# Reordering in three places of a two-layer sparse-attention block: x tiles turned earlier, one softmax moved, casts held

## The chip, the cores and the metric

The kernel runs on one core of a Trainium2 chip. The metric is the device time of one execution in microseconds (us); the time before is the median of three runs, 749.46 us (749.03 to 749.6). The core has a matrix engine (TensorE; PE in the profile, PEld for its weight loads), VectorE (DVE), ScalarE (ACT), GpSimd (POOL) and a queue that issues most DMAs (SP). GpSimd issues DMAs too, among them the accumulating ones. Each engine takes its instructions in the order of its own queue.

## The reference

Two layers are applied to 528 tokens (16 meta tokens and 512 of x) of width 1024. Each projects the normalised tokens to several parts, lets an indexer choose 128 keys for each query, attends to these, adds a pooled branch, gates both and adds an output product to its input:

```
def hybrid_layer(x, ...):
    h = rms_norm(x, norm_g)
    proj = h @ w_in           # q, k, v, gate_a, u_b, gate_b, q_idx, k_idx, w_idx, merge
    q = rope(rms_norm(q)); k = rope(rms_norm(k)); q_idx = rope(q_idx); k_idx = rope(k_idx)
    score = sum_heads(relu(q_idx . k_idx) * w_idx)        # keys after the query's chunk left out
    sel   = the 128 best keys of each query
    attn  = softmax(q . k[sel] / 8) @ v[sel]              # 8 heads, one k and v
    y_a = (attn * silu(gate_a)) @ w_a
    y_b = (pool(u_b) * silu(gate_b)) @ w_b
    g_a, g_b = sigmoid(merge)
    return x + (g_a * y_a + g_b * y_b) @ w_out
```

Only the 512 tokens of x are returned.

## The kernel before, in words

**Precision.** Matrix products run in a fast format that rounds its inputs. To keep the precision, an operand is split into a high part (a cast, on ScalarE) and a low part (the difference, on VectorE or GpSimd), and each product is three: high by high, high by low, low by high. So each chunk of weights needs casts (`w<-raw`) and subtractions (`w<-raw,w`) before its product; raw weights lie in four buffers, split ones in eight. The state of the tokens is kept transposed: `RES` (channels by tokens), its normalised form `NF`, and the split form `hhi`, `hlo`.

**Order of the work.** TensorE's and VectorE's instructions stand in the order in which the program issues them. ScalarE's, GpSimd's and SP's order is chosen by a planner, which estimates when each could run; `tc.issue_after(x)` makes it put an instruction behind `x`. The program issues its groups of matmuls one after the other, and after each group `group_done()` (from line 357) issues what is due: items put off with `later(fn, n)` until n groups are over, one item of weight preparation (`prep_q`), and steps of `fill`, a queue of Python generators that holds the index scores and the attention. A generator's `yield` ends a step. So where a `yield` stands in the attention decides between which matmul groups an instruction comes.

**The start.** x arrives in four tiles of 128 tokens (`xt`), the first two at once, the last two (t = 3, 4) issued behind the first weights. `x_half` takes their sums of squares (ScalarE), and GpSimd makes `rstd`, the reciprocal root. `x_turned` (16 transposes for the last two tiles, into banks `a`) fills `RES`. `norm_half` turns `rstd` along the tokens with two more transposes and multiplies, which gives eight blocks `nf` on VectorE, then `hhi` (ScalarE) and `hlo`. In layer 0 the first three tiles (meta, 1, 2) go ahead: keys and values of these (`plain_trio`), index queries of tile 1 (`tok_group`, 24 matmuls), *then* the transposes of tiles 3 and 4, a fold of the meta keys, index queries of tile 2, with the second `norm_half` in the middle of its matmuls (`hooks[1]`), and then keys of tile 3 and 4 (`plain_group`), which read `nf` straight.

**Attention.** `attention` (from line 746) works on 16 units u = 4i + j: query tile i (0 to 3), two heads each. `logits(u)` makes scores on TensorE into the four banks `a`; `soft(u)` adds the mask on VectorE, which reads the scores out of the banks (`lt<-a,sc`), takes the running minimum `mn`, and then takes the exponential on ScalarE (L780); `scale(u)` normalises; `turn(u)` transposes, into banks `a` again; `values(u)` multiplies by v. The steps run between the matmul groups of the gates' products (`mix_gates`). For u of 13 and above, `soft(u)` is issued in the same step as `logits(u)`, below that one step later. Unit 12 is the first of the last query tile, whose scores take two banks for each head, so all four.

**Products of seven.** The gates and part of the last output product run as `group_of_products` (from line 979): a 2 x 2 block product in seven products instead of eight, with sums of the inputs (`sums_of_h`, `sums_of_merged`) and of the weights (`mixed_prep`, nine items i0 to i8: casts, low parts, sums on VectorE, and an accumulating DMA `raw<-s` from GpSimd). The seven products are a11, a12, s2, s1, s3, s4, a22 in turn, over three banks `d`. After the first, ScalarE copies the bank out (`p`) before the third may add to it.

**The end.** In layer 1, the products with `w_a` give `ta`; its sum with `zb` is cast to `hhi` (L1405). `rows(c, t, w)` computes one tile of 128 tokens by 256 output channels: two transposes of `RES`, a copy `rt` of these (L1479), 24 matmuls, and on VectorE the sum `ot`, which a DMA writes out. Column block 0 and three tiles of block 1 are done so; the sums for the last two blocks are made meanwhile: `first`, `sums` and `lows` for each of four k, and `fourth`, `last_high` and `last_low`, whose result is wanted only by the seventh product (a22). Then `mix_out` runs two groups of seven products, with the last `rows` between.

Of the kernel before, what the change touches and what calls it, by code (L numbers as in the profile page):

```python
# [36 lines left out]
LAG1 = 2  # L37
# [53 lines left out]
def tile_block(ctx: ExitStack, tc: tile.TileContext, x, meta, w_in, pool_w, w_a, w_b, w_out, rows, hgain, c_tab, out):  # L91
    nc = tc.nc
    act, gp = nc.scalar, nc.gpsimd
# [149 lines left out]
        else:  # L243
            prep_q.extend((lambda: high(0), second, lambda: low(1)))

    added = [None]

    def first_sum(c):
        if c in mixed:
# [2 lines left out]
    def mixed_prep(c):  # L252

        r0, r1 = raws[c]
        blk = {"a11": r0[:, 0], "a21": r0[:, 1], "a12": r1[:, 0], "a22": r1[:, 1]}
        src = {"a11": "a11", "a12": "a12", "a22": "a22", "s3": "a21", "s2": "s2", "s1": "a11", "s4": "a12"}
        ops = ready[c]

        def hi(n):
            t = w_tile().rearrange("p (s k e) -> p s k e", s=2, k=4)  # L260
            ops[n] = t
            act.copy(t[:, 0], blk[src[n]])  # L262

        def lo(n):
            dve.tensor_sub(ops[n][:, 1], blk[src[n]], f(ops[n][:, 0]))

        def i0():
            hi("a12")

        def i1():  # L270
            lo("a12")
            blk["s2"] = tmp.tile([128, 544], F32, tag="L", name="s2", bufs=LB)[:, :512].rearrange(
                "p (k e) -> p k e", k=4)
            dve.tensor_add(blk["s2"], blk["a21"], blk["a22"])
            gp.dma_start(blk["a12"], blk["s2"], accum_op=OP.add)  # L275
            hi("a11")

        def i2():
            lo("a11")
            dve.tensor_sub(blk["a11"], blk["s2"], blk["a11"])  # L280

        def i3():
            hi("s2")

        def i4():
            lo("s2")
            hi("s1")

        def i5():
            lo("s1")  # L290
            hi("s3")

        def i6():
            lo("s3")
            hi("s4")
            first_sum(c + 1)

        def i7():
            lo("s4")
            hi("a22")  # L300

        def i8():
            lo("a22")
            del raws[c]
            w_load()

        def counted(fn):
            def item():
                fn()
                progress[c] += 1  # L310
            return item

        progress[c] = 0
        return [counted(fn) for fn in (i0, i1, i2, i3, i4, i5, i6, i7, i8)]
# [19 lines left out]
    def later(fn, n=2):  # L334
        pend.append((count[0] + n, fn))
# [410 lines left out]
    def attention(ensure, later_rate):  # L746
# [95 lines left out]
        for u in range(-1, 17):  # L842
            while u == 4 and not SIL["ready"]:
                yield
            if u == 7:
                rate[0] = later_rate
            if u + 1 < 16:
                logits(u + 1)
            if 0 <= u < 16:
                scale(u)  # L850
            if 13 <= u + 1 < 16:
                soft(u + 1)
            yield
            if u + 1 < 13:
                soft(u + 1)
            if u >= 1:
                turned.append(u - 1)
                if u % 4 == 0 or (u > 8 and u % 2 == 0):
                    while turned:
                        values(turned.pop(0))  # L860
                if u % 4 == 0:
                    meta_values(u // 4 - 1)
            yield
            if u >= 1 and u % 4 == 0:
                gated(u // 4 - 1)
            if 0 <= u < 16:
                turn(u)
                if u % 4 == 3:
                    meta_turn(u // 4)
            yield  # L870
# [280 lines left out]
    rstd = one.tile([128, 5], F32, name="rstd0")  # L1151
# [39 lines left out]
    tp = bank("d")  # L1191
# [7 lines left out]
    dve.tensor_scalar(psc, parT[:, 24:32], 0.5, None, op0=OP.mult)  # L1199
    dve.tensor_reduce(fold, ident.rearrange("p (j c) -> p c j", j=4), axis=AX.X, op=OP.add)  # L1200
    tables(0, True)
    hooks = {0: lambda: None, 1: lambda: ends.append(norm_half(0, 1, rstd, LAG1))}
    ends = []

    for l in range(2):
# [16 lines left out]
        w = chunk()  # L1222
        W["use"] += 1
        if l == 0:
            squared = x_half(1, halved)
        for t in (1, 2):
            later(lambda t=t, ps=pss[t]: kv_post(l, t, ps), 1)
        later(lambda ps=pss[0]: meta_sum(ps, KV, lambda total: kv_post(l, 0, total)), 1)
# [1 line left out]
        for what, t in (("q", 1), ("q", 2), ("k", 3), ("k", 4), ("q", 3), ("q", 4)):  # L1230
            if what == "k":
                ps = plain_group(t, raws[kv])
                later(lambda t=t, ps=ps: kv_post(l, t, ps), 1)
            else:
                index_queries(t, 0, w, hooks[1] if (l, t) in ((0, 2), (1, 1)) else None)
                if (l, t) == (0, 1):
                    x_turned(1, squared)
            group_done()
            if (what, t) == ("k", 3):
                w_prep_enqueue(True, None if l else ends[0])  # L1240
            if (what, t) == ("k", 4):
                del raws[kv]
                w_load()
# [228 lines left out]
        else:  # L1472
            def rows(c, t, w, half=lambda: None):
# [2 lines left out]
                for b in range(2):  # L1476
                    pe.transpose(tp[:, b * 128:(b + 1) * 128], RES[0][:, 2 * c + b, s:s + 128], ident)
                rt = tmp.tile([128, HB], F32, tag="tt", name="rt", bufs=6)
                act.copy(rt[:, :256], tp[:, :256])  # L1479
                ps = bank("d")  # L1480
                steps = [(jj, k) for k in range(KT) for jj in range(3)]
                if c == 0 and t == 1:
# [17 lines left out]
            w = chunk()  # L1500
            for t in range(1, 4):
                rows(1, t, w)
            for k in range(4):
                fourth(k)
                last_high(k)
            later(lambda: [last_low(k) for k in (0, 1)], 2)
            later(lambda: [last_low(k) for k in (2, 3)], 3)
            mix_out(operands)
            rows(1, 4, w, flush)

# [51 lines left out]
```

## Time and profile before

| | |
|---|---|
| median of three runs | 749.46 us |
| profiled execution | 749.96 us, of which the span (first to last instruction) 748.1 |
| busy: TensorE, its weight loads | 735.4 us (98%), 705.9 (94%) |
| busy: VectorE, ScalarE, GpSimd | 589.5 (79%), 482.3 (64%), 243.9 (33%) |
| DMA | 106.41 MB, 142 GB/s on average |
| granted TensorE clock | 0.999 of full speed |

A row of the timeline gives the start (us), the duration, engine, line, operation, `out<-in` by the program's names, the shape, a count where neighbours are merged, and in brackets how long the engine was idle before and what ended that. Line 62 is a helper through which all instructions of TensorE and VectorE go, so these are told apart by their tiles. A row of the list of waits gives who waited for whom: us in total, times, the longest.

### The profile page before, as it was taken

What the parts mean: (1) busy time and instruction counts of PE and PEld (TensorE: products, weight loads), DVE (VectorE), ACT (ScalarE), POOL (GpSimd) and SP (SyncE); (2) the same over time, 40 slices, a digit from 0 to 9 for tenths busy, and PEclk for the clock granted to TensorE, in tenths of its full rate; (3) what the DMA queues carried; (4) which work ended last, traced back from release to release, by engine and by line L of the source; (5) the groups of instructions that cost most, each with busy time, mean ns of one, the idle gap of its engine ahead of it and who ended that gap; (6) DMA issues with size and microseconds to landing.
All of it is one profiled execution on the core that took longest, in us unless ns stands there. A gap on an engine that the chain in (4) does not pass through costs nothing.

```text
span 748.1 us, 16060 instructions
## 1 busy us (share of the span) xinstructions
PE 735.4 (98%) x5949; PEld 705.9 (94%) x5949; DVE 589.5 (79%) x1500; ACT 482.3 (64%) x1099; POOL 243.9 (33%) x320
## 2 busy tenths in 40 slices
PE   9999999999999999999999999999999999999998
PEld 8899998999999999999999989998899999999997
DVE  6876998998898785794358669999989977678674
ACT  6669745657688786543245796557577877865543
POOL 3642074721222211063346411755031231106200
PEclk9999999999999999999999999999999999999999
DMA  8766764964654523643422687669364644548732
GB/s 264 229 169 159 167 143 113 229 147 93 146 110 116 124 59 99 179 149 115 142 87 85 173 179 195 154 153 220 84 141 108 140 93 91 128 122 241 182 88 71
DMA packets 103566, 106.41 MB, mean 142 GB/s; under 512 B 5008, under 2 KB 83632, under 8 KB 103488
## 3 DMA queue, kind: packets, MB, share of 16 engines
q1 hardware_dynamic: 91888, 74.89, 33.1%
q0 software_dynamic: 11520, 30.41, 22.8%
q8 instruction: 46, 0.75, 0.4%
q14 instruction: 32, 0.26, 0.1%
q10 hardware_dynamic: 80, 0.08, 0.0%
HBM read 66.41 MB, written 8.55 MB: 100 GB/s over the span
## 4 chain that ended last, share of the span: by engine, by line
PE 71%; DVE 14%; ACT 5%; DMA 5%; issue 2%; POOL 1%; SPq 1%; DVEq 0%; POOLq 0%; ACTq 0%
PE d L62 57%; PE a L62 10%; PE v L62 4%; DVE sc L62 3%; DVE w L62 2%; DVE m L62 2%; DMA xt<-in_x_dram 2%; DMA raw<-in_w_out_dram 1%; ACT lt L780 1%; ACT w L262 1%; DMA raw<-s 1%; DVE t L62 1%; DMA w<-raw 1%; DVE s L62 1%; POOL hlo L1407 1%
## 5 line engine op out<-in xcount | busy, mean ns | idle before, releaser
L62 PE MATMUL d<-hhi,w 128*128 128x256 f32 (+3 forms) x1392 | 279.3, 292 | 1.3 <-DVE w L62 0.7
L62 PEld LDWEIGHTS d<-hhi,w 128*128 128x128 f32 x1392 | 222.3, 188 | 5.6 <-DVE w L62 1.6
L62 PE MATMUL d<-hlo,w 128*128 128x256 f32 (+3 forms) x696 | 189.8, 289 | 0.0
L62 PEld LDWEIGHTS d<-hlo,w 128*128 128x128 f32 x696 | 131.2, 189 | 1.4 <-issue 0.2
L62 DVE TENSOR_TENSOR w<-raw,w 128x512 fp32r<-128x512 f32 (+1 forms) x156 | 120.7, 784 | 3.9 <-ACT w L262 3.9
L62 PE MATMUL d<-hsum,w 128*128 128x264 f32 (+1 forms) x720 | 95.4, 285 | 0.5 <-ACT p L1006 0.4
L62 PEld LDWEIGHTS d<-hsum,w 128*128 128x128 f32 x720 | 89.4, 188 | 1.5 <-ACT p L1006 0.8
L262 ACT CAST w<-raw 128x512 fp32r<-128x512 f32 x132 | 76.5, 622 | 18.0 <-DVE raw L62 9.5
L62 PE MATMUL d<-w,hhi 128*128 128x256 f32 x576 | 86.1, 287 | 1.4 <-ACT hhi L1405 1.1
L62 PEld LDWEIGHTS d<-w,hhi 128*128 128x128 f32 x576 | 74.7, 188 | 6.3 <-ACT hhi L1405 1.3
L250 POOL DMA_DIRECT2D raw<-raw x22 | 19.9, 903 | 117.8 <-DMA raw<-in_w_in_dram 66.6
L62 DVE MATCH_REPLACE8 sc<-m,sc 128x400 f32<-128x400 f32 (+2 forms) x100 | 54.3, 548 | 0.0
L220 POOL DMA_DIRECT2D w<-raw x34 | 31.6, 945 | 68.6 <-ACT w L219 46.2
L62 DVE MAX8 m<-sc 128x8 f32<-128x400 f32 (+2 forms) x100 | 52.6, 556 | 0.8
L275 POOL DMA_DIRECT2D raw<-s x22 | 19.3, 875 | 84.9 <-issue 23.4
L780 ACT ACTIVATE lt<-lt,mn,NR 128x144 f32<-128x144 f32 (+3 forms) x64 | 42.3, 664 | 6.3 <-DVE mn L62 6.0
L62 DVE SCALAR_TENSOR_TENSOR sc<-r,wsg,sc 128x144 f32<-128x144 f32 (+3 forms) x56 | 32.4, 582 | 17.3 <-ACT r L704 15.0
L62 PE MATMUL d<-w,hlo 128*128 128x256 f32 x288 | 45.7, 281 | 0.0
L62 PE MATMUL d<-mhi,w 128*128 128x272 f32 (+2 forms) x192 | 45.3, 324 | 0.0
L1407 POOL TENSOR_TENSOR hlo<-ta,hhi 128x256 fp32r<-128x256 f32 (+1 forms) x28 | 26.8, 966 | 46.6 <-PE d L62 34.4
L795 POOL TENSOR_SCALAR pm<-lt,rs 128x16 f32<-128x16 f32 x48 | 24.5, 549 | 52.5 <-DVE rs L62 47.9
L667 POOL TENSOR_TENSOR t<-t,t 128x256 f32<-128x256 f32 (+1 forms) x34 | 32.1, 944 | 28.5 <-DVE t L62 28.2
(245 smaller groups left out, 1560.6 us busy)
## 6 DMA issues: line engine op xcount, KB each, us to landing
raw<-in_w_in_dram SPq DMA_DIRECT2D x88, 256.0 KB, 3.5
w<-raw POOLq DMA_DIRECT2D x34, 512.0 KB, 5.9
raw<-in_w_in_dram SPq DMA_DIRECT2D x32, 512.0 KB, 4.5
raw<-in_w_out_dram SPq DMA_DIRECT2D x12, 512.0 KB, 3.7
raw<-raw POOLq DMA_DIRECT2D x22, 256.0 KB, 4.0
raw<-s POOLq DMA_DIRECT2D x22, 256.0 KB, 3.3
kept<-res SPq DMA_DIRECT2D x16, 264.0 KB, 2.5
res<-kept SPq DMA_DIRECT2D x16, 264.0 KB, 6.1
```

What stands on the lines that cost most here:

```text
L62: return fn(*a, **k)
L220: gp.dma_start(t, raws[c][s], accum_op=OP.add)
L250: gp.dma_start(raws[c][0][:, 1], raws[c][0][:, 0], accum_op=OP.add)
L262: act.copy(t[:, 0], blk[src[n]])
L275: gp.dma_start(blk["a12"], blk["s2"], accum_op=OP.add)
L667: added[0] = gp.tensor_tensor(t1[:m, :256], t1[:m, :256], t2[:m, :256], op=OP.add).ins
L780: act.activation(L[hh][:, :n], L[hh][:, :n], AF.Exp, scale=NR[:, i, h:h + 1], bias=mn[:, hh:hh + 1], accum_out=sm[:, hh:hh + 1])
L795: (gp if j < 3 else dve).tensor_scalar(pms[i][:, 2 * j + hh, :], L[hh][:, 0:16], rs[:, hh:hh + 1], None, op0=OP.mult)
L1407: pool_end = gp.tensor_sub(hlo[:, j, a:a + n], d, f(hhi[:, j, a:a + n]))
```

## The change

1. **x tiles.** In layer 0 `x_turned(1, ...)` (the 16 transposes) is issued directly after `x_half`, ahead of the first index queries. `norm_half(0, 1, ...)` is issued right after these queries and no longer inside the second ones.
2. **Softmax.** The bound in `attention` goes from 13 to 12: `soft(12)` is issued in the step of `logits(12)`, in both layers. On VectorE its four passes and the product on `mn` come ahead of a sum `c`, a low part `w` and a subtraction of the weight preparation.
3. **Casts.** `mixed_prep`'s casts are put behind `mark[0]` on ScalarE, the latest `rt` copy of `rows` at the time of issue. Ahead of the first `rows` there is no mark, so it bears on the last two chunks of `w_out` alone.
4. **Sums.** `fourth`, `last_high` and `last_low` of the last product are put off with `later`: `fourth` and the first two `last_high` to the end of the first of the seven products, the other two by one more, and the `last_low` by one more than before each. On ScalarE as built, `p` of the first product now comes behind one cast of `last_high` where it came behind four.

On SP, the first output write now stands ahead of the last chunk's loads, and the second ahead of the last of them. No instruction is added or removed on any engine.

```diff
-    added = [None]
+    added, mark = [None], [None]
...
         def hi(n):
             t = w_tile().rearrange("p (s k e) -> p s k e", s=2, k=4)
             ops[n] = t
-            act.copy(t[:, 0], blk[src[n]])
+            with tc.issue_after(mark[0]) if mark[0] else nullcontext():
+                act.copy(t[:, 0], blk[src[n]])
...
-            if 13 <= u + 1 < 16:
+            if 12 <= u + 1 < 16:
                 soft(u + 1)
             yield
-            if u + 1 < 13:
+            if u + 1 < 12:
                 soft(u + 1)
...
-    hooks = {0: lambda: None, 1: lambda: ends.append(norm_half(0, 1, rstd, LAG1))}
+    hooks = {0: lambda: None}
...
         if l == 0:
-            squared = x_half(1, halved)
+            x_turned(1, x_half(1, halved))
...
-                index_queries(t, 0, w, hooks[1] if (l, t) in ((0, 2), (1, 1)) else None)
+                index_queries(t, 0, w, hooks[1] if (l, t) == (1, 1) else None)
                 if (l, t) == (0, 1):
-                    x_turned(1, squared)
+                    ends.append(norm_half(0, 1, rstd, LAG1))
...
-                act.copy(rt[:, :256], tp[:, :256])
+                mark[0] = act.copy(rt[:, :256], tp[:, :256]).ins
...
-            for k in range(4):
-                fourth(k)
-                last_high(k)
-            later(lambda: [last_low(k) for k in (0, 1)], 2)
-            later(lambda: [last_low(k) for k in (2, 3)], 3)
+            later(lambda: [fourth(k) for k in range(4)], 1)
+            later(lambda: [last_high(k) for k in (0, 1)], 1)
+            later(lambda: [last_high(k) for k in (2, 3)], 2)
+            later(lambda: [last_low(k) for k in (0, 1)], 3)
+            later(lambda: [last_low(k) for k in (2, 3)], 4)
             mix_out(operands)
```

## The prediction

> **What bounds the kernel now.** I read the page's first part, then the list of waits of TensorE's weight loads (PEld), because every matmul starts with one, and then the timeline around each long wait.
>
> ```profile
> span 748.1 us, 16060 instructions
> PE 735.4 (98%) x5949; PEld 705.9 (94%) x5949; DVE 589.5 (79%) x1500; ACT 482.3 (64%) x1099; POOL 243.9 (33%) x320
> ...
> PEld d L62 <- ACT p L1006: 2.7, 5, 1.2
> PEld a L62 <- DVE mn L62: 2.0, 2, 1.0
> ...
> PEld d L62 <- ACT hhi L1405: 1.3, 1, 1.3
> ```
>
> TensorE is busy for 98% of the span, so the time is its work plus its waits, and an edit counts only where it makes or removes a wait of TensorE. The change adds no instruction and removes none on TensorE, VectorE, ScalarE or GpSimd; it only reorders. Three waits in the list lie exactly where it does so: on `mn` (twice, once a layer), on `hhi` (once) and on `p` (the 1.2). The first 30 us are the fourth place.
>
> **Part A, the last x tiles turned first.** The weight loads, then the landings of the two tiles (the chain of waits and the DMA view of 8 to 9.5 us), the reciprocal root on GpSimd, and the first and last normalised block:
>
> ```profile
> 10.45 5.37 PEld L62 LDWEIGHTS d<-raw,nf 128*128 128x128 f32 x32 [0.28 <-DVE nf L62]
> ...
> 16.87 1.01 PEld L62 LDWEIGHTS d<-w,hhi 128*128 128x128 f32 x8 [0.32 <-ACT w L205]
> ...
> 19.72 1.77 PEld L62 LDWEIGHTS a<-consts,xt 128*128 128x128 f32 x16
> 21.83 0.11 PEld L62 LDWEIGHTS a<-part,fold 128*16 128x16 f32 x2 [0.34 <-ACT res L1187]
> 22.27 1.01 PEld L62 LDWEIGHTS d<-w,hhi 128*128 128x128 f32 x8 [0.33 <-DVE res L62]
> ...
> 25.52 1.02 PEld L62 LDWEIGHTS d<-raw,nf 128*128 128x128 f32 x6
> ...
> 29.48 0.70 PEld L62 LDWEIGHTS v<-raw,nf 128*128 128x128 f32 x4
> ```
>
> ```profile
> 8.36 2.57 SPq L424
> 10.97 8.42 DMA xt<-in_x_dram
> ...
> xt<-in_x_dram SPq DMA_DIRECT2D x1, 512.0 KB, 8.6
> ```
>
> ```profile
> 21.45 0.72 POOL L485 TENSOR_TENSOR rstd<-rstd,mhalf 128x2 f32<-128x2 f32 x1
> ...
> 24.94 1.24 DVE L62 SCALAR_TENSOR_TENSOR nf<-res,parT,a 128x256 f32<-128x256 f32 x3
> ...
> 28.69 0.46 DVE L62 SCALAR_TENSOR_TENSOR nf<-res,parT,a 128x256 f32<-128x256 f32 x1
> ```
>
> Before, the 24 loads of the first index queries (16.87 to 19.72, 2.85 us) cover the time until the last tile lands at 10.97 + 8.42 = 19.39. After, TensorE's queue has the 16 transposes first. The first eight can start when their tile lands, 8.36 + 8.6 = 16.96; at 1.77 / 16 = 0.11 each they end at 17.84. The other eight wait until about 19.47: a new wait of 1.6 us, with the index queries queued behind it. They end at 20.35 and the queries at 23.20.
>
> What it buys: the two turns of `rstd` now stand right behind these queries. `rstd` exists at 22.17, so the normalised blocks start at about 23.6 instead of 24.94 (the small keys' work on VectorE goes behind them), and with the old spacing of 4.2 us (24.94 to 29.15) the last is there at 27.8. The fold, the second queries and the turns need 0.11 to 0.44 (its waits gone or not) and 3.25 (22.27 to 25.52), so the third tile's 16 plain loads start at 26.6 to 26.9. Without waits they take 16 x 5.37 / 32 = 2.69, where they took 25.52 to 29.48 = 3.96 while waiting for the blocks. They need the last block seven eighths through, at 28.9: no wait is left. They end at 29.3 to 29.6 against 29.48. I take a gain of 0.1. Ends: a loss of 1.6 if the old waits stay, a gain of 0.5 if the fold's wait and some latency vanish too. On SP the copies of x to `kept` wait for the turned tiles and start a little earlier; nobody waits for them. The keys' splits on VectorE come 1 us later, but their transposes follow only behind the fourth tile's loads (2.7 us more), so I cost that at nothing; without this cover it would be 1 us.
>
> The longer wait also raises the clock. The nearest row is the stretch with the longest idle of TensorE after the first microseconds, and its granted clock (third number from the end) stayed 1.00:
>
> ```profile
> 694.00:700.00 6.00, 4.88 (x40) 4.52 (x39) 1.82 (x5) 1.94 (x4) 1.49 (x2) 1.00 0.59 140
> ```
>
> So by the rows an idle of 1.3 us costs nothing. [...]
>
> **Part B, the last tile's first softmax ahead of the yield.** VectorE and then PEld of layer 0:
>
> ```profile
> 263.42 0.42 DVE L62 TENSOR_TENSOR c<-d,u 128x264 f32<-128x264 f32 x1
> 263.76 0.68 DVE L62 TENSOR_TENSOR w<-raw,w 128x512 fp32r<-128x512 f32 x1
> ...
> 265.09 0.43 DVE L62 CUSTOM_DVE_ANT_0 lt<-a,sc 128x272 f32<-128x272 f32 x1
> ...
> 266.98 0.16 DVE L62 TENSOR_TENSOR mn<-mn,RQ 128x2 f32<-128x2 f32 x1
> ```
>
> ```profile
> 265.58 0.73 PEld L62 LDWEIGHTS a<-consts,lt 128*128 128x128 f32 x6 [1.02 <-DVE mn L62]
> ...
> 266.83 0.31 PEld L62 LDWEIGHTS d<-hhi,w 128*128 128x128 f32 x2
> ```
>
> The transposes wait for a score bank that the first `lt<-a,sc` frees. After, this block (265.09 to 267.1, 2.0 us) runs at 263.42, the bank is free at 263.9 and the wait of 1.0 us is gone. But the sum `c`, the weight split `w` and a subtraction now queue behind the block. The split is the low half of the next product's weights: it ended at 264.4, and will at 266.4. TensorE wants it at its third load, 266.83 before; from 264.56, where the wait began, that is 1.27 us of work later, 265.8. It will wait until about 266.5, so the gain here is 0.3 and not 1.0. Ends: 0 (exponentials now stand ahead of weight casts on ScalarE) and 1.0.
>
> Layer 1, where the scores are loaded, what VectorE waits for, and the same wait:
>
> ```profile
> 620.74 1.04 PEld L62 LDWEIGHTS a<-KK,qq 128*128 128x128 f32 x8
> ...
> 623.51 0.43 DVE L62 TENSOR_TENSOR c<-d,p 128x256 f32<-128x256 f32 x1 [3.16 <-PE d L62]
> ...
> 625.55 0.73 PEld L62 LDWEIGHTS a<-consts,lt 128*128 128x128 f32 x6 [0.94 <-DVE mn L62]
> ```
>
> Here VectorE is idle for 3.16 us ahead of `c`. The scores come from 620.74 on, so the block runs from about 621.1 to 623.1, inside that idle time, and delays nothing: gain 1.0 (ends 0.7 and 1.0).
>
> **Part C, casts held and sums spread.** VectorE, ScalarE and PEld around 698 us:
>
> ```profile
> 694.31 0.59 DVE L62 TENSOR_TENSOR ta<-ta,zb 128x256 f32<-128x256 f32 x1
> ```
>
> ```profile
> 698.06 0.62 ACT L262 CAST w<-raw 128x512 fp32r<-128x512 f32 x1 [4.30 <-DMA raw<-in_w_out_dram]
> 698.58 0.40 ACT L1405 CAST hhi<-ta 128x256 fp32r<-128x256 f32 x1
> ```
>
> ```profile
> 697.52 0.19 PEld L62 LDWEIGHTS d<-w,hlo 128*128 128x128 f32 x1
> 699.03 0.30 PEld L62 LDWEIGHTS d<-w,hhi 128*128 128x128 f32 x2 [1.32 <-ACT hhi L1405]
> 699.49 0.19 PEld L62 LDWEIGHTS d<-w,hlo 128*128 128x128 f32 x1 [0.16 <-DVE hlo L62]
> ```
>
> The input of the last `hhi` cast is ready at 694.90, but ScalarE stands 4.30 us in front of it on a weight cast whose data has not landed, and TensorE waits. In the changed order that cast (and the second one like it) stands behind the copies `rt` of the last product's rows, where its data is long there. `hhi` then runs at 694.95, and its low half on VectorE at 695.4. The wait goes: three load starts took 1.97 us (697.52 to 699.49) instead of 3 x 0.12, a gain of 1.6. What is late next is the second half's `hhi`, behind two weight casts; only the third row group wants it, and before it came later and still in time, so I cost it at nothing. VectorE's sums start about 3 us earlier, with the `hhi` casts (698.58 before, 694.95 after), so they no longer lag behind TensorE. Ends: 1.3 and 1.6.
>
> Around 721 us: ScalarE, the load that waits, GpSimd's accumulating DMA, and its landing in the chain.
>
> ```profile
> 718.78 1.66 ACT L262 CAST w<-raw 128x512 fp32r<-128x512 f32 x3 [0.66 <-DMA raw<-s]
> 720.35 1.32 ACT L1106 CAST osum<-ta 128x256 fp32r<-128x256 f32 x4
> 721.58 0.36 ACT L1006 COPY p<-d 128x256 f32<-128x256 f32 x1
> ...
> 721.99 0.19 PEld L62 LDWEIGHTS d<-osum,w 128*128 128x128 f32 x1 [1.21 <-ACT p L1006]
> ...
> 715.07 0.86 POOL L275 DMA_DIRECT2D raw<-s  x1 [3.56 <-DMA out_dram<-ot]
> ...
> 715.07 3.69 DMA raw<-s
> ```
>
> After, `p` follows the first of the four `osum` casts: three of 0.33 go behind it, 1.0 of the 1.21. The rest comes from the DMA, whose source no longer lags (above), so that it lands earlier against TensorE. I take 1.2; ends 0.8 and 1.3. `osum`'s low halves go behind `c` and `res` on VectorE; they are needed four products later (over 5 us).
>
> The queues that are passed: SP now issues the first output write before the last chunk's loads, and the second before the last of these. The writes wait for `ot`, which comes earlier. Cost nothing.
>
> **Sum.** 0.1 + 0.3 + 1.0 + 1.6 + 1.2 = 4.2 us. The profiled run took 749.96 (span and 1.86 around it), so it would be 745.8; the median stands 0.5 lower, so 749.46 - 4.2 = 745.3.
>
> **Rivals.**
>
> 1. *`p` stays late* (746.5). ScalarE reaches `p` only through the cast that waits for `raw<-s`. With TensorE 1.6 us earlier and this landing not, the wait at 721.99 stays. For it: the [0.66 <-DMA]. Against: its source follows VectorE. 749.46 - 3.0.
> 2. *The x tiles cost* (747.0). The 1.6 us wait appears and the blocks are not earlier, because VectorE or ScalarE reaches them no sooner. 749.46 - 4.2 + 1.7. [...] I give that 0.02 of this rival's chance.
> 3. *Slower: the last sum on GpSimd comes late* (751 or more). GpSimd's `raw<-s` stands behind the last chunk's first accumulation, whose loads are the ones that SP now holds behind an output write. If that write's `ot` were held, loads, both accumulations, the cast, `p` and the product all follow. Once it lands later than the 1.2 us gained at `p` allow, each microsecond costs one: it decides from about 5.4 us late on (4.2 + 1.2), and is 0.2% slower at 7. Against: `ot` waits only for a finished row group.
> 4. *Nothing changes* (749): another wait behind each takes over, as VectorE at 79% could. Against: layer 1's idle 3.16 and ScalarE's 4.30.
>
> **How the numbers follow.** Forecast 0.60, rival 1 0.16, rival 2 0.13, rival 3 0.06, rival 4 0.05. The forecast's own ends are 744.0 (layer 0 whole, A's best) and 746.3. The range reaches over rivals 1 and 2 to 747.4 and leaves 0.11 and the spread outside. A measurement tells 0.2%, 1.5 us, from no change: faster 0.88, same 0.05, slower 0.07.
>
> **What would show it.** In the profile after: the transposes of `xt` at 17 and at 19.5 with a wait of 1.6 between, and loads of `d<-raw,nf` without waits on `nf`; no PEld wait on `mn`; a new wait on VectorE's `w` of about 0.7 near 266; no 4.30 at ScalarE's cast and no wait on `hhi` near 698; `p` ahead of three `osum` casts, no wait on it there. A wait on `raw<-s` or on `nf` of over 1 us makes me wrong.

## The result, and the profile after

The changed kernel takes 745.01 us (median of six runs, 744.77 to 746.29), against 749.36 for the kernel before in the same comparison (six runs): a ratio of 0.9947, 95% interval 0.9934 to 0.996, or 4.0 us less (3.0 to 4.9). Predicted were 4.2 less and 745.3. The profiled execution took 745.0, with a span of 743.1 against 748.1, so the two profiles differ by 5.0.

The page's first part and the list of waits of the weight loads, of the kernel after:

```profile
span 743.1 us, 16072 instructions
PE 733.4 (99%) x5949; PEld 706.4 (95%) x5949; DVE 590.3 (79%) x1500; ACT 482.0 (65%) x1099; POOL 243.9 (33%) x320
...
PEld d L62 <- DVE w L62: 2.7, 5, 1.1
...
PEld d L62 <- ACT p L1007: 1.6, 4, 0.7
...
PEld a L62 <- ACT KI L642: 0.8, 2, 0.5
```

The waits on `mn` and on `hhi` are out of the list, and that on `p` is no longer 1.2 at its longest. Two rows are worth a look: the wait on `w`, now 1.1 at its longest (0.7 before), and a wait of 0.5 on `KI` (0.2 before). Each engine has as many instructions as before; the 12 more in the page's total (16072 against 16060) are waits for semaphores, which the page does not count as busy.

Where the 5.0 us lie is seen by following the same weight load through both traces. The lead of the kernel after over the one before, from rows shown here or in the prediction and others like them:

| from, to (before; after) | before | after | gained |
|---|---|---|---|
| span's start to the key transposes `a<-identr,ks` (48.13; 47.27) | 48.13 | 47.27 | 0.86 |
| to the scores `a<-KK,qq` of layer 0's unit 12 (260.61; 259.84) | 212.48 | 212.57 | -0.09 |
| to those of unit 13 (268.04; 267.14): part B, layer 0 | 7.43 | 7.30 | 0.13 |
| to unit 12 of layer 1 (620.74; 619.82) | 352.70 | 352.68 | 0.02 |
| to unit 13 (629.37; 627.23): part B, layer 1 | 8.63 | 7.41 | 1.22 |
| to the last load of the row `d<-osum,w` at 728.09; 723.13 (729.39; 724.42): part C | 100.02 | 97.19 | 2.83 |
| to the end | 18.71 | 18.68 | 0.03 |

The start: one weight load of the kernel before, then of the kernel after the weight loads, the last tile's square on ScalarE and the first normalised block on VectorE:

```profile
48.13 0.39 PEld L62 LDWEIGHTS a<-identr,ks 128*128 128x128 f32 x4 [0.22 <-ACT KI L641]
```

```profile
17.31 1.73 PEld L62 LDWEIGHTS a<-consts,xt 128*128 128x128 f32 x16 [0.32 <-issue]
...
25.50 2.68 PEld L62 LDWEIGHTS d<-raw,nf 128*128 128x128 f32 x16
28.16 2.73 PEld L62 LDWEIGHTS v<-raw,nf 128*128 128x128 f32 x16
...
47.27 0.39 PEld L62 LDWEIGHTS a<-identr,ks 128*128 128x128 f32 x4 [0.50 <-ACT KI L642]
```

```profile
18.16 1.06 ACT L1171 ACTIVATE start<-xt 128x1024 f32<-128x1024 f32 x1
...
22.34 1.26 DVE L62 SCALAR_TENSOR_TENSOR nf<-res,parT,a 128x256 f32<-128x256 f32 x3 [0.95 <-PE a L62]
```

The 16 transposes run in one piece: no wait of 1.6 stands among them. The last x tile was there by 18.1, where it had landed at 19.39 before. The 16 plain loads stand in one row of 2.68, without waits on `nf`, as predicted; they end at 28.16, 1.3 earlier than before. Of this lead 0.46 is gone at 47.27, where TensorE waits for ScalarE's `KI`.

Layer 0, VectorE and the weight loads:

```profile
262.66 0.43 DVE L62 CUSTOM_DVE_ANT_0 lt<-a,sc 128x272 f32<-128x272 f32 x1
...
264.24 0.48 DVE L62 CUSTOM_DVE_ANT_0 lt<-a,sc,mn 128x256 f32<-128x256 f32 x1
...
264.85 0.42 DVE L62 TENSOR_TENSOR c<-d,u 128x264 f32<-128x264 f32 x1
265.19 0.68 DVE L62 TENSOR_TENSOR w<-raw,w 128x512 fp32r<-128x512 f32 x1
```

```profile
263.75 0.69 PEld L62 LDWEIGHTS a<-consts,lt 128*128 128x128 f32 x6
264.40 0.14 PEld L62 LDWEIGHTS a<-consts,pm 128*128 128x128 f32 x1
...
265.93 0.30 PEld L62 LDWEIGHTS d<-hhi,w 128*128 128x128 f32 x2 [1.11 <-DVE w L62]
```

The transposes `a<-consts,lt` no longer wait, and two loads after `pm` TensorE waits 1.11 for the split `w`, which ends at 265.87 behind the four passes and `c`.

Layer 1, the same two engines: the first pass runs while VectorE was idle, and the transposes start without a wait.

```profile
620.38 0.44 DVE L62 CUSTOM_DVE_ANT_0 lt<-a,sc 128x272 f32<-128x272 f32 x1 [0.94 <-PE a L62]
```

```profile
623.65 0.68 PEld L62 LDWEIGHTS a<-consts,lt 128*128 128x128 f32 x6
```

The end, ScalarE, then the two places where TensorE had waited:

```profile
692.82 0.41 ACT L1406 CAST hhi<-ta 128x256 fp32r<-128x256 f32 x1 [1.18 <-DVE ta L62]
...
713.36 2.82 ACT L263 CAST w<-raw 128x512 fp32r<-128x512 f32 x5 [0.75 <-DVE raw L62]
716.09 0.40 ACT L1107 CAST osum<-ta 128x256 fp32r<-128x256 f32 x1
716.39 0.36 ACT L1007 COPY p<-d 128x256 f32<-128x256 f32 x1
716.66 1.02 ACT L1107 CAST osum<-ta 128x256 fp32r<-128x256 f32 x3
```

```profile
695.52 0.31 PEld L62 LDWEIGHTS d<-w,hhi 128*128 128x128 f32 x2
...
717.02 2.90 PEld L62 LDWEIGHTS d<-osum,w 128*128 128x128 f32 x24
```

The last `hhi` waits only for its own input, the five casts of `w` stand in one row where one of them had waited for `raw<-s`, and `p` comes ahead of three `osum` casts. Neither `d<-w,hhi` nor `d<-osum,w` has a wait.

### The profile page after: what moved, and what is told of

Read it like the earlier page. It is cut to its first block, busy times and chain, and to the rows that moved or that the text cites. A ratio compares the mean times of both kernels' runs of the same rounds, so it can differ in the third digit from the quotient of the medians.

```text
span 743.1 us, 16072 instructions
## 1 busy us (share of the span) xinstructions
PE 733.4 (99%) x5949; PEld 706.4 (95%) x5949; DVE 590.3 (79%) x1500; ACT 482.0 (65%) x1099; POOL 243.9 (33%) x320
## 4 chain that ended last, share of the span: by engine, by line
PE 74%; DVE 17%; ACT 5%; issue 2%; POOL 2%; DVEq 0%; POOLq 0%; ACTq 0%
PE d L62 60%; PE a L62 10%; PE v L62 4%; DVE w L62 3%; DVE sc L62 3%; DVE m L62 2%; DVE t L62 2%; ACT lt L781 1%; DVE lt L62 1%; ACT w L263 1%; DVE s L62 1%; DVE zb L62 1%; ACT lt L795 1%; DVE c L62 1%; DVE raw L62 1%
## 5 line engine op out<-in xcount | busy, mean ns | idle before, releaser
L668 POOL TENSOR_TENSOR t<-t,t 128x256 f32<-128x256 f32 (+1 forms) x34 | 32.4, 954 | 28.3 <-DVE t L62 26.9
```

Source lines behind the costliest of these rows:

```text
L668: added[0] = gp.tensor_tensor(t1[:m, :256], t1[:m, :256], t2[:m, :256], op=OP.add).ins
```

## The experiments

Each kernel ran beside the kernel before on the same chip, but not all on one chip; where the chips differ, the ratios compare and the medians only roughly. The times, with the ratio to the kernel before and its 95% interval:

| kernel | median us | ratio | span profiled |
|---|---|---|---|
| the changed kernel | 745.01 | 0.9947 (0.9934 to 0.996) | 743.1 |
| part A alone | 749.99 | 1.0009 (0.9997 to 1.0022) | 747.6 |
| part B alone | 747.58 | 0.9972 (0.9962 to 0.9982) | 745.5 |
| casts held alone | 747.21 | 0.9969 (0.9955 to 0.9982) | 745.3 |
| sums put off alone | 748.41 | 0.9981 (0.997 to 0.9992) | 746.4 |
| B and C, without A | 745.02 | 0.9947 (0.9935 to 0.996) | 742.8 |
| changed kernel, last tile late | 746.67 | 0.9979 (0.9967 to 0.9991) | 744.6 |
| B and C, last tile late | 745.55 | 0.9951 (0.9936 to 0.9966) | 744.1 |
| changed kernel, B in layer 1 only | 745.97 | 0.9958 (0.9945 to 0.9971) | 743.5 |
| changed kernel, passes two and two | 745.67 | 0.9951 (0.9937 to 0.9964) | 742.7 |
| changed kernel, three and one | 744.44 | 0.9939 (0.9923 to 0.9954) | 742.9 |
| B and C, two and two | 744.63 | 0.9945 (0.9931 to 0.9958) | 742.7 |
| B and C, three and one | 743.68 | 0.9929 (0.9917 to 0.9941) | 741.8 |

An interval is some 2 us wide, so a step of less than 1 us is read from the rows.

### Part A alone

```diff
-    hooks = {0: lambda: None, 1: lambda: ends.append(norm_half(0, 1, rstd, LAG1))}
+    hooks = {0: lambda: None}
...
-            squared = x_half(1, halved)
+            x_turned(1, x_half(1, halved))
...
-                index_queries(t, 0, w, hooks[1] if (l, t) in ((0, 2), (1, 1)) else None)
+                index_queries(t, 0, w, hooks[1] if (l, t) == (1, 1) else None)
                 if (l, t) == (0, 1):
-                    x_turned(1, squared)
+                    ends.append(norm_half(0, 1, rstd, LAG1))
```

> The kernel before with part A alone (last x tiles turned ahead of the first index queries, the normalised half behind them). Theory from the profile of after: the last tile's 16 transposes run at about 17.3 to 19.1 without a long wait, because the last x tile lands at about 18.1; the fourth tile's plain loads start 0.9 to 1.3 us earlier than before and 0.8 to 0.9 us of that is still there at the end: 0.8 to 0.9 us faster. Rival, the prediction's term: the tile lands at 19.4, a wait of about 1.6 stands in front of the second eight transposes, and the gain is 0.1. Rival, the x tiles cost: 1.6 us slower.

Measured: 749.99, ratio 1.0009: no gain. The weight loads of its trace:

```profile
17.02 0.86 PEld L62 LDWEIGHTS a<-consts,xt 128*128 128x128 f32 x8 [0.32 <-ACT sq L599]
19.49 0.86 PEld L62 LDWEIGHTS a<-consts,xt 128*128 128x128 f32 x8 [1.61 <-DMA xt<-in_x_dram]
...
29.50 1.54 PEld L62 LDWEIGHTS v<-raw,nf 128*128 128x128 f32 x9
```

This is the picture that the prediction drew: a wait of 1.61, transposes at 19.49, the fourth tile at 29.50 against 29.48 before. My new theory, taken from the one trace of the changed kernel, fell; the prediction's own term held here. Each engine's instructions stand in the same order in both traces; what differs is when the last x tile landed. In every trace without an added copy (a later experiment adds one), the last of that load's completion events, the start of the key transposes near 47, and the time between the two (us):

| order of the x tiles | landing | key transposes | between |
|---|---|---|---|
| old: sums put off alone | 17.96 | 47.47 | 29.50 |
| old: B and C, three and one | 18.16 | 46.91 | 28.74 |
| old: part B alone | 18.31 | 47.05 | 28.75 |
| old: B and C | 18.42 | 47.18 | 28.77 |
| old: B and C, two and two | 18.51 | 47.27 | 28.77 |
| old: casts held alone | 19.00 | 47.75 | 28.75 |
| old: the kernel before | 19.39 | 48.13 | 28.74 |
| new: two and two | 18.04 | 47.18 | 29.14 |
| new: the changed kernel | 18.08 | 47.27 | 29.20 |
| new: B in layer 1 only | 18.30 | 47.45 | 29.14 |
| new: three and one | 18.39 | 47.54 | 29.15 |
| new: part A alone | 19.45 | 48.59 | 29.15 |

Both orders met early and late landings. In both, the key transposes follow the landing one to one (with one exception, the earliest tile, where something else came last). At the same landing the new order is behind, by 0.4. So the 0.86 of the table above is a landing that came 1.31 earlier (18.08 against 19.39), less about 0.45 that part A costs.

### Parts B and C without part A

```diff
-            x_turned(1, x_half(1, halved))
+            squared = x_half(1, halved)
...
                 if (l, t) == (0, 1):
-                    ends.append(norm_half(0, 1, rstd, LAG1))
+                    x_turned(1, squared)
```

(and `hooks[1]` back in the second index queries)

> The changed kernel without part A (parts B and C alone). Theory after the run of part A alone: part A is worth nothing by itself (0 to +0.5 us over many runs), and the early start seen in the one profile of the changed kernel was the last x tile landing at 18.1 where it landed at 19.4 before; so this kernel takes 744.6 to 745.4, within 0.5 us of the changed kernel. Rival, part A gained the 0.9 us that the two profiles show: 745.9 or more. Rival, it costs by its wait: 743.9 or less. The last tile's landing in the old order gets another sample: the fourth tile's first plain loads start at 28.4 to 28.8 if it lands at 18.0 to 18.3, at 29.1 to 29.5 if at 19.0 to 19.4.

Measured: 745.02, equal to the changed kernel's 745.01. Its weight loads at the start:

```profile
27.11 0.69 PEld L62 LDWEIGHTS d<-raw,nf 128*128 128x128 f32 x4 [0.38 <-DVE nf L62]
28.23 0.30 PEld L62 LDWEIGHTS d<-raw,nf 128*128 128x128 f32 x2 [0.43 <-DVE nf L62]
28.51 2.73 PEld L62 LDWEIGHTS v<-raw,nf 128*128 128x128 f32 x16
...
47.18 0.40 PEld L62 LDWEIGHTS a<-identr,ks 128*128 128x128 f32 x4 [0.24 <-ACT KI L642]
```

The old order still waits twice for `nf` and reaches the fourth tile at 28.51 against 28.16; at the key transposes it is level (47.18 against 47.27), though its tile landed 0.34 later. There the wait on `KI` is 0.24, against 0.50 in the new order. ScalarE makes `KI` at 46.75 and 46.84 in the two traces, behind two weight casts: it sets the time, and TensorE's lead is spent waiting for it. Followed further back, ScalarE waits for GpSimd and GpSimd for VectorE. In the new order this leads to VectorE's key work, which runs from 26.97 to 31.02 right behind the eight blocks. GpSimd there, then in the old order:

```profile
31.10 0.85 POOL L668 TENSOR_TENSOR t<-t,t 128x256 f32<-128x256 f32 x1 [0.79 <-DVE t L62]
...
35.01 0.87 POOL L477 TENSOR_TENSOR Cg<-consts,gains 128x320 f32<-128x320 f32 x1 [0.50 <-DVE t L62]
```

```profile
34.91 0.88 POOL L477 TENSOR_TENSOR Cg<-consts,gains 128x320 f32<-128x320 f32 x1 [0.96 <-DVE t L62]
```

Behind the landing, GpSimd's `Cg` comes 16.93 in the new order and 16.49 in the old one: the same 0.4 as at the key transposes. So part A removes the waits on `nf` (three of 0.43 in the kernel before) and gains nothing by it. By time none of the pairs shows a gain either: 745.01 with part A and 745.02 without, 745.67 and 744.63 with the passes split two and two, 744.44 and 743.68 with three and one.

### The last tile made late, in both orders

```diff
     for t in range(2, 4):
+        if t == 3:
+            dma(spare_rows, x[0, 0:128, :])
         dma(xt[:, t, :], x[0, t * 128:(t + 1) * 128, :])
```

In the changed order:

> The changed kernel with a copy of 512 KB of x from DRAM to DRAM issued between the loads of the last two x tiles, so that the last tile lands later by about 1 to 1.6 us. Theory: in the new order TensorE stands directly behind this landing, so every microsecond after 18.1 appears as a wait in front of the second eight transposes (landing at 19.5: 1.6; at 21: 3.1) and at least nine tenths of it is still there at the fourth tile's plain loads: 1 to 2 us slower than the changed kernel. Rival, the landing is hidden behind VectorE's and ScalarE's work on the tiles: 0 to 0.3 slower.

The copy goes to a spare DRAM tile that nothing reads. Measured: 746.67, 1.7 more than without it. The load that waits and the key transposes:

```profile
19.91 0.86 PEld L62 LDWEIGHTS a<-consts,xt 128*128 128x128 f32 x8 [2.09 <-DMA xt<-in_x_dram]
...
48.99 0.39 PEld L62 LDWEIGHTS a<-identr,ks 128*128 128x128 f32 x4 [0.51 <-ACT KI L645]
```

The tile landed at 19.87, 1.8 later than in the changed kernel's trace, and the key transposes start 1.7 later, 29.11 behind the landing. Nothing hides the landing.

In the old order (B and C without A):

> Parts B and C without A, with the copy of 512 KB between the loads of the last two x tiles that made the last tile land at 19.9 in the changed order. Theory: in the old order the first index queries stand in front of the transposes and TensorE comes to them at about 19.7, so a landing at 19.9 costs 0.2 to 0.3 there, and what VectorE and ScalarE then do later costs up to 1.2 more at the normalised blocks: 0.3 to 1.3 slower than the version without the copy, against 1.7 in the changed order. Rival, the old order hides a late tile wholly: 0 to 0.2. Rival, it is hit as the new one: 1.6 or more.

Measured: 745.55, 0.5 more than without the copy. The tile landed even later, at 20.71, and yet:

```profile
19.81 1.80 PEld L62 LDWEIGHTS a<-consts,xt 128*128 128x128 f32 x16
...
48.35 0.40 PEld L62 LDWEIGHTS a<-identr,ks 128*128 128x128 f32 x4 [0.22 <-ACT KI L645]
```

The key transposes start at 48.35, 1.2 later than without the copy (47.18), for a tile that is 2.3 later (20.71 against 18.42); no load of `xt` shows a wait on the DMA. It looks as if the 24 loads of the index queries hid a part of the lateness. The table above says otherwise: these loads stand there in all traces of the old order, and from 18.42 to 19.39 a tile that was 0.97 later cost 0.95. What is different here is the order on ScalarE and GpSimd, which the planner chose anew with the copy in the program. ScalarE in the kernel before, then in this run:

```profile
19.48 1.06 ACT L1170 ACTIVATE start<-xt 128x1024 f32<-128x1024 f32 x1 [1.29 <-DMA xt<-in_x_dram]
...
20.54 0.20 ACT L599 ACTIVATE sq<-d 128x64 f32<-128x64 f32 x1
```

```profile
17.78 0.20 ACT L603 ACTIVATE sq<-d 128x64 f32<-128x64 f32 x1
...
20.80 1.06 ACT L1174 ACTIVATE start<-xt 128x1024 f32<-128x1024 f32 x1 [0.86 <-DMA xt<-in_x_dram]
```

In the old order ScalarE stands right behind the landing, with the square of the last tile; that is why a late tile costs this order too. With the copy, small work of the keys (`sq` and others) went ahead of the square, and two `rk` of GpSimd ahead of `rstd`. The first block `nf` then starts 4.45 behind the landing, where it starts 5.55 behind it in the six traces above. That this order saved the 1.1 is read from the rows; no run has it without the copy. So the two late runs do not compare the two orders of the x tiles.

### Part B alone, and in layer 1 alone

```diff
-            if 13 <= u + 1 < 16:
+            if 12 <= u + 1 < 16:
                 soft(u + 1)
             yield
-            if u + 1 < 13:
+            if u + 1 < 12:
                 soft(u + 1)
```

> The kernel before with part B alone (the last tile's first softmax ahead of the yield). Theory: in layer 0 the wait of 1.0 on mn goes and a wait of 1.1 on VectorE's w comes a microsecond later, gain 0 to 0.1; in layer 1 the wait goes and nothing takes its place, gain 1.0 to 1.2: together 1.0 to 1.3 us faster. Rival, the prediction's size: the new wait in layer 0 is 0.7 only, gain 0.3 there and 1.3 together. Rival, each layer gains its whole wait: 2.0. Its start is that of before, so it also shows once more where the last x tile lands in the old order (19.4 in the one profile of before).

Measured: ratio 0.9972, or 2.1 us less (1.3 to 2.9). From the scores of unit 12 to those of unit 13, layer 0 takes 7.28 (7.43 before) and layer 1 7.41 (8.63): 1.37 together, which lies inside the interval. The two profiles differ by 2.6; of the rest 1.08 is there at the key transposes, by an early x tile in this trace (18.31). Its row of layer 0 repeats the new wait:

```profile
265.58 0.30 PEld L62 LDWEIGHTS d<-hhi,w 128*128 128x128 f32 x2 [1.11 <-DVE w L62]
...
719.48 2.85 PEld L62 LDWEIGHTS d<-osum,w 128*128 128x128 f32 x24 [1.66 <-ACT p L1006]
```

The second row shows rival 1 of the prediction at work where part C is missing: TensorE comes 3.0 earlier to the end of the `hhi` wait, but `p` only 2.5 earlier, and the wait on `p` grows from 1.21 to 1.66.

With the changed kernel's bound put back to 13 in layer 0 only (`attention(..., 13 - l)`, and `early` for 12):

> The changed kernel with part B in layer 1 alone (in layer 0 the last tile's first softmax stands behind the yield, as before). Theory: layer 0 was worth nothing, so this is within 0.1 us of the changed kernel in the profile (the wait on mn of 1.0 is back near 265, the wait on w of 1.1 is gone) and within 0.4 in the timed median. Rival, the prediction's 0.3 for layer 0: 0.3 slower. Rival, the new wait costs more than the old: 0.2 to 0.5 faster.

Measured: 745.97, 1.0 more than the changed kernel by medians from different comparisons (ratios 0.9958 and 0.9947, whose intervals overlap). By its rows layer 0 takes 7.44 from unit 12 to 13, against 7.30: the move is worth 0.14 there. The old wait is back and the new one gone, as expected:

```profile
265.09 0.73 PEld L62 LDWEIGHTS a<-consts,lt 128*128 128x128 f32 x6 [1.02 <-DVE mn L62]
266.04 0.14 PEld L62 LDWEIGHTS a<-consts,pm 128*128 128x128 f32 x1 [0.22 <-issue]
```

Another 0.18 stands at the key transposes, where the tile landed 0.22 later. The rest of the timed 1.0, more than the 0.4 expected, stays open.

### The passes of layer 0 split around the weight work

```diff
-            if 12 <= u + 1 < 16:
+            if u + 1 == 12 and not split_rest:
+                soft(12, slice(0, 2))
+            elif 12 <= u + 1 < 16:
                 soft(u + 1)
             yield
-            if u + 1 < 12:
+            if u + 1 == 12 and not split_rest:
+                soft(12, slice(2, None))
+            elif u + 1 < 12:
                 soft(u + 1)
```

(`soft` does the passes named, and takes `mn` and the exponentials after the last; `split_rest` is the layer's number)

> The changed kernel, but in layer 0 only the first two of the last tile's four VectorE passes stand ahead of the yield; the other two follow the sum c, the weight split w and a subtraction. Layer 1 as in the changed kernel. Theory (the gain of layer 0 was eaten because the split w stood behind all four passes): c at about 263.7, w at 264.0 to 264.7, ahead of TensorE's third load, so the wait of 1.1 on w goes and none comes back on mn: 1.0 faster than the changed kernel, 5.2 to 5.5 faster than the kernel before. Rival, the exponentials become the bound as they move back by a microsecond: a wait near 267 takes the place, 0 to 0.3 faster than the changed kernel. Rival, the bank is freed by the later passes: the wait on mn is back and nothing is won.

Measured: 745.67, no faster than the changed kernel, and in layer 0 7.08 from unit 12 to 13 against 7.30: a gain of 0.2 where 1.0 was expected. The wait on `w` is gone, and this stands in its place, one consumer earlier:

```profile
265.24 0.14 PEld L62 LDWEIGHTS a<-consts,pm 128*128 128x128 f32 x1 [0.96 <-issue]
```

All four banks had held scores, and two passes free only two. As I read it, the six transposes fill these, and the seventh, of `pm`, needs a third bank: its matmul starts at 265.27, after ScalarE's first copy out of one (`pt<-a`, 264.55 to 265.12). None of the expectations had named this consumer. The same edit on B and C without A:

> Parts B and C without A, with the last tile's passes in layer 0 split two and two. Theory: the same 1.0 us on top of the version without part A: 743.6 to 744.4. Rival: as above, the exponentials become the bound and it ends within 0.3 of that version.

Measured: 744.63, 0.4 less than 745.02, and 7.07 in layer 0: the same. Then three passes ahead and one behind (`slice(0, 3)`, `slice(3, None)`), in the changed kernel:

> The changed kernel, but in layer 0 three of the last tile's four VectorE passes stand ahead of the yield and one behind the sum c, the split w and a subtraction. Theory: the split by two and two only moved the wait to the next consumer, the one transpose of pm, whose bank the third pass frees. With three passes ahead all banks are free in time; c follows at 264.2, w ends at 265.3, and TensorE, which wants it at 264.8, waits 0.5 in place of 1.1: 0.5 to 0.6 faster than the changed kernel in the profile (the stall near 265 of 1.2 shrinks to 0.6). Rival, any order of these passes costs about 1 us because VectorE has 2.7 us of them and the sum in front of it: the stall stays at 1.0 to 1.2, at whichever consumer.

Measured: 744.44, and 6.44 in layer 0, 0.86 less than in the changed kernel and more than the 0.6 expected. The split `w` now runs on VectorE from 264.61 to 265.29. The load of `pm`, and the load that wants `w`:

```profile
264.65 0.14 PEld L62 LDWEIGHTS a<-consts,pm 128*128 128x128 f32 x1
...
265.34 0.30 PEld L62 LDWEIGHTS d<-hhi,w 128*128 128x128 f32 x2 [0.28 <-DVE w L62]
```

No wait on a bank, and 0.28 left on `w`. This fits the reading above: the third pass had freed the bank. The rival that VectorE's work costs 1 us in any order is out. Last, the same without part A:

> Parts B and C without A, with three of the last tile's four passes of layer 0 ahead of the yield: the best order by the runs so far. Theory: 0.6 to 0.9 us faster than parts B and C without A and with all four passes ahead (745.0), since the stall near 265 shrinks from 1.2 to 0.35, and 0 to 0.3 faster than the same split with part A (744.4), since part A brings nothing: 744.1 to 744.5. Rival, part A is worth something once layer 0 no longer stalls: 744.7 or more.

Measured: 743.68, the lowest of all, 5.3 us under the kernel before (4.4 to 6.2) and below the expected 744.1. Layer 0 takes 6.44 again (259.35 to 265.79). It is 1.3 below the changed kernel in median, and the intervals overlap a little (up to 0.9941, and from 0.9934); the rows of layer 0 bear out 0.86 of it, and those of the key transposes another 0.36 (46.91 against 47.27).

### The casts held alone, and the sums put off alone

```diff
-            act.copy(t[:, 0], blk[src[n]])
+            with tc.issue_after(mark[0]) if mark[0] else nullcontext():
+                act.copy(t[:, 0], blk[src[n]])
...
-                act.copy(rt[:, :256], tp[:, :256])
+                mark[0] = act.copy(rt[:, :256], tp[:, :256]).ins
```

> The kernel before with the casts of the last product's sums held behind the rows' copies, and nothing else. Theory that the two halves of part C hang together: the wait of 1.3 on hhi near 698 goes (gain 1.6), VectorE's sums follow earlier, so the accumulating DMA of the last sums is issued and lands earlier, and the wait of 1.2 on p near 721 shrinks to about 0.4 although four osum casts are still ahead of p: 2.3 to 2.6 us faster. Rival, two independent parts: 1.6 faster, the wait on p stays at 1.2 or grows by what TensorE gains. Rival, another wait takes over: 0 to 0.5.

Measured: ratio 0.9969, 2.3 us less (1.3 to 3.4); by its trace 2.34 between the load at 649.72 before (649.28 here) and that at 729.39 (726.61). ScalarE and the load that still waits:

```profile
714.97 2.71 ACT L263 CAST w<-raw 128x512 fp32r<-128x512 f32 x5 [0.68 <-DVE raw L62]
717.58 1.32 ACT L1107 CAST osum<-ta 128x256 fp32r<-128x256 f32 x4
```

```profile
719.22 2.89 PEld L62 LDWEIGHTS d<-osum,w 128*128 128x128 f32 x24 [0.46 <-ACT p L1007]
```

The cast no longer waits for `raw<-s`: the accumulating DMA is issued at 712.30, 2.8 earlier than before (715.07), and `p` comes 2.8 earlier too (718.81 against 721.58). TensorE comes 2.0 earlier to this load (718.76 against 720.78). The difference takes the wait on `p` from 1.21 to 0.46, though four `osum` casts are still in front of it. The other half:

```diff
-            for k in range(4):
-                fourth(k)
-                last_high(k)
-            later(lambda: [last_low(k) for k in (0, 1)], 2)
-            later(lambda: [last_low(k) for k in (2, 3)], 3)
+            later(lambda: [fourth(k) for k in range(4)], 1)
+            later(lambda: [last_high(k) for k in (0, 1)], 1)
+            later(lambda: [last_high(k) for k in (2, 3)], 2)
+            later(lambda: [last_low(k) for k in (0, 1)], 3)
+            later(lambda: [last_low(k) for k in (2, 3)], 4)
```

> The kernel before with the last sums put off and spread, the casts not held. Theory: the wait on hhi of 1.3 stays; p stands behind one osum cast less three, so of its wait of 1.2 about 0.8 to 1.0 goes, but the part that the landing of the accumulating DMA sets stays (0.2 to 0.4): 0.8 to 1.0 us faster. Rival: p is held by the landing alone and nothing changes, 0. Rival: the whole wait goes, 1.2.

Measured: ratio 0.9981, 1.4 less (0.6 to 2.2); by its trace 0.82 between the same loads (648.90 to 727.75). The cast still waits for the landing, and `p` behind it:

```profile
718.06 1.66 ACT L262 CAST w<-raw 128x512 fp32r<-128x512 f32 x3 [0.82 <-DMA raw<-s]
```

```profile
720.35 2.90 PEld L62 LDWEIGHTS d<-osum,w 128*128 128x128 f32 x24 [0.65 <-ACT p L1006]
```

Each half alone leaves a part of the wait on `p` (0.46 and 0.65 of 1.21); both together leave none. Alone they gain 2.34 and 0.82 by the traces, together 2.83 and not 3.16, since both take from this one wait.

## Why the prediction was right, and where it was not

**The sum.** 4.2 predicted, 4.0 measured (3.0 to 4.9), and the terms B and C carry it. By the rows of the table they come to 0.13 + 1.22 + 2.83 = 4.18, against the predicted 0.3 + 1.0 + 2.8 = 4.1; part A comes to a loss of 0.4 at the same landing, against a gain of 0.1. That the two profiles differ by 5.0 is luck: the tile was late in the one and early in the other. The forecast's own upper end, 746.3, is not the sum of the lower ends given with the terms (-1.6 + 0 + 0.7 + 1.3 + 0.8 = 1.2, which would be 748.3); nothing here hung on it.

**Part A.** Up to 30 us the picture was right for a tile that lands at 19.4. In part A alone the blocks start at 23.68 (23.6 forecast), the third tile's loads at 26.84 (26.6 to 26.9) and end at 29.50 (29.3 to 29.6). Two steps were wrong.

The first is "the other eight wait until about 19.47: a new wait of 1.6 us". That took the landing at 19.39 from one trace as if it were fixed by the issue. Over twelve traces without the extra copy it was between 17.96 and 19.45; the wait is 1.61 in one kernel, 0.3 in three and none in the changed one. In "what would show it" I named that wait as a mark of the step, and its absence proves nothing. The DMA's count of completions shows where the lateness lies: in the three late traces the last event stands 0.9 to 1.3 behind the one before it (18.18, then 19.39 in the kernel before), in the others 0.5 at most. Why that last event was late was not tried. The clock, which the longer wait brought up, did not fall: part A alone, with its wait of 1.61, had a mean granted clock of 1.0 over its profiled execution, and so had the changed kernel with the late tile, with its wait of 2.09. The 0.02 within rival 2 is the chance of a slower clock behind this wait; no run shows one, and these two clocks are what was measured.

The second is the keys' splits, which "I cost at nothing" because their transposes follow only behind the fourth tile's loads. These transposes did not wait, as forecast (30.87 in the changed kernel, right behind the loads). But the same key work on VectorE, now behind the blocks, also holds up GpSimd, and through it ScalarE's `KI` at 47 us. There the new order is 0.4 later at the same landing (29.15 behind it against 28.75). The prediction's reckoning stopped at 30 us. In rival 2 (the x tiles cost) the 1.6 us wait was right for a late tile, and the rest was not: the blocks did come earlier, 4.23 behind the landing against 5.55, and the price was 0.4 and not 1.7.

**Part B, layer 0.** The mechanism was as predicted, "the sum `c`, the weight split `w` and a subtraction now queue behind the block"; the size was off by 0.17. The term that failed is the new wait, 0.7 forecast and 1.11 measured. Counted from unit 12's scores, TensorE wanted `w` 0.3 sooner than I had it, since a small stall behind the old wait went too (`pm` stood 0.37 behind `lt` where 0.11 is usual, seen again in the run with part B in layer 1 only as [0.22 <-issue]; by the reading of the banks above, `pm` waited for the third pass, which ended at 266.42); and `w` came 0.2 later, since the block with its product took 2.19 (262.66 to 264.85) and not 2.0.

**Part B, layer 1.** Predicted 1.0, measured 1.22: the wait on `mn` (0.94) and the same small stall behind it. My upper end was 1.0. The passes ran at 620.38 to 622.5, in the idle time of VectorE as forecast.

**Part C.** Predicted 1.6 + 1.2, measured 2.83 together. The claim on which the 1.2 hung, that the accumulating DMA follows VectorE's earlier sums, is borne out by the casts held alone: its issue moved by 2.8, VectorE's sum `s` in front of it ended 3.0 earlier (711.77 against 714.77), and the wait fell to 0.46 with nothing done to the order at `p`. In these two traces an output write lands between `s` and the issue, and the profile names that as what ended GpSimd's wait; in the changed kernel it names `s`:

```profile
710.63 0.86 POOL L276 DMA_DIRECT2D raw<-s  x1 [3.43 <-DVE s L62]
```

Rival 1 is what happens without it (1.66 with part B alone).

**Rivals 3 and 4.** GpSimd's sum came earlier and not late; another wait took over in two of the four places, on `w` in layer 0 and on `KI` behind the x tiles.

## What to carry to other kernels

A landing seen in one trace is a sample (here 17.96 to 19.45 over twelve): look at it in several traces, and compare two orders by the time from the landing to a later instruction. Here one profile of each order showed 0.86 in favour of the one that, at the same landing, costs 0.4. When an instruction block moves ahead of others on its engine, list every consumer of what it now stands in front of, those on other engines included, and every resource that each piece of the block frees; here TensorE waited 1.11 for the split weight behind four passes and 0.96 at the transpose of `pm` behind two, and the best cut was between the third and fourth pass, with no wait at `pm` and 0.28 left on the split weight. Look also for a cast that waits for a DMA: in the kernel before, one stood 4.30 on ScalarE until its data had landed, with `hhi` behind it, whose input was ready at 694.90 and which ran at 698.58. With the casts held and nothing else, a later transfer came forward as well: the accumulating DMA was issued 2.8 earlier.

## What the runs showed that I had not expected

The load of the last x tile, 512 KB, issued at 10.67 to 11.29 us into the span as the second of a pair, landed 1.23 to 1.25 behind the first of the pair in nine of twelve traces, and 2.12 to 2.57 behind it in three. Neither its issue (10.88 to 10.97 in these three) nor the order of the work that waits for it tells which. And single passes counted at the score banks: with two of the four passes of layer 0 ahead, the transpose of `pm`, whose load takes 0.14 us, waited 0.96, and with three it did not wait.
